# A hybrid decoder trunk in float32: the GLA gate inputs stacked as high and low parts on partitions, and the gate logits formed by two rounded products

## The chip, the cores and the metric

The kernel runs on one core of one Trainium2 chip. The metric is device time of one execution in microseconds (us); lower is better. The engines are named as the profile names them: PE is TensorE (matrix products, with PEld its weight loads), DVE is VectorE, ACT is ScalarE, POOL is GpSimd, SP is SyncE, which here only issues DMAs. POOL issues DMAs too.

## The reference, cut to what matters

One layer with three branches that read the same normalised rows. Only the gated linear attention (GLA) branch is touched by the change, and of it only the forget gate:

```python
h = rmsnorm(x, norm_gain)
proj = h @ w_in                                   # one combined projection
q, k, v, gla_g, a_lr, u, pool_g, xq, xg, merge = jnp.split(proj, split_pts, axis=-1)
z = (a_lr @ w_a2 + b_a).astype(jnp.float32)       # a_lr: (B, T, 16), w_a2: (16, 512)
log_a = (jax.nn.log_sigmoid(z) / GATE_TAU).reshape(B, T, GLA_HEADS, GLA_DK)
o, S = gla_chunked(q, k, v, log_a, S0)            # 4 heads of key width 128
```

There are 1024 prompt rows and 8 sample rows. The gate input a_lr has rank 16 and the logits z have 512 columns, 128 for each of the four heads. All tensors are float32.

## The kernel before

The order of the work on PE and of the DMAs that SP issues is that of the program text. The instructions of ACT, DVE and POOL are put in order when the kernel is compiled, by a scheduler with a cost model of its own; on the chip each engine then runs its list in that fixed order.

**The main stream.** The combined projection is cut into 36 pairs of column blocks. A pair is worked as seven products; each is 2 column halves x 4 inner steps x 3 matmuls of 128x258 (`product`, with `mm3` at L242 to L244). mm3 multiplies float32 operands as high part times high part, high times low and low times high, all in the rounded type fp32r; ACT makes the high part (L223) and DVE the low part (L224). After the pairs come 24 units of the branch projections and then the output projection.

**The side stream.** After every half of a product `fill` takes steps from generators: first the memory projection, then cross attention (`cross_steps`, 16 steps of `s` and two to drain), then GLA (`gla_steps`, 16 chunks of 256 columns), then pooling. Each `yield` carries a cost by which the side work is spread over the main stream, so that PE always has something to run.

**The gate.** `small_loads` fetches the 16 columns of w_in that give a_lr into `wa`, which has 32 columns of which 16 were set to zero, and copies w_a2 four times into `w2`, 128x512, at partitions 32j to 32j+15. `gate_half` multiplies `wa` with the normalised rows into four groups of 32 output partitions, one group for every fourth inner block, so that its 128 partitions hold four partial sums of a_lr. They go to DRAM (`al_scr`) for the prompt and into `als` for the samples. Later `gla_load` fetches a chunk of them as `alc`, and one plain float32 matmul of `w2` with `alc` adds the four partial sums and multiplies by w_a2 at once (L907, 16 times; L1012 for the samples, 4 times):

```python
nc.tensor.matmul(t[:, :CT], lhsT=w2[:, h * P:(h + 1) * P], rhs=alc, start=True, stop=True)
gate_exps(t[:, :CT], CT, h, z, b)
```

**What sets the order around the change.** Three stores of buffers matter. `R` gives 2 KB tiles from a ring of 14 (`NR`) that nearly all small work shares: cross attention's queries, their high parts, probabilities `p`, transposed probabilities `pT`, outputs `xo`, memory tiles. `E` gives 30 (`NE`) larger tiles, 28 of which hold the operands of the main stream during the pairs. `PX` and `PZ` are PSUM tiles of the main and side stream. In cross attention, step s runs `cross_scores(s)`, then `cross_values(s-2)`, then `cross_weights(s-1)`, so that what a step makes is used one step later. POOL's list holds the stores of results to DRAM: `xo` at L737, `c` at L593 with the copy of the sample columns at L569 before it, `mkv` at L457 and L458.

Of the kernel before, what the change touches and what calls it, by code (L numbers as in the profile page):

```python
# [9 lines left out]
F32 = mybir.dt.float32  # L10
F32R = mybir.dt.float32r
# [3 lines left out]
AF = mybir.ActivationFunctionType  # L15
ALU = mybir.AluOpType
AX = mybir.AxisListType

P = 128
D = 1024  # L20
T = 1024
NS = 8
# [25 lines left out]
def trunk_kernel(ctx: ExitStack, tc: tile.TileContext,  # L48
# [65 lines left out]
    def R(shape, dt=F32, name="r"):  # L114

        return shaped(wk.tile([P, 512], dt, tag="ring", name=name, bufs=NR), shape)
# [68 lines left out]
    nc.vector.memset(pm, 0.0)  # L185
    qm = pm[:, 0]

    w2 = cp.tile([P, 512], F32, name="w2")
    nc.vector.memset(w2, 0.0)
    ssq = cp.tile([P, 16], F32, name="ssq")  # L190
    nc.vector.memset(ssq, 1.0)

    smp = cp.tile([P, 33 * NS], F32, name="smp")
    brs = [cp.tile([P, NK, NS], F32, name=f"brs{n}") for n in range(3)]
    als = cp.tile([P, NS], F32, name="als")
    S_XQ, S_Q, S_K, S_V, S_U = 0, 8, 12, 16, 24

    def smp_of(j, n=1):
# [2 lines left out]
    def scratch(n, name, shape):  # L201
        return [dr.tile(list(shape), F32, name=f"{name}{i}") for i in range(n)]
# [3 lines left out]
    acc_scr = [scratch(NK, f"acc{n}_", (P, TT)) for n in range(2)]  # L206
    mkv_scr = [scratch(NH, f"mkvs{o}", (P, 2, DV)) for o in range(2)]
    al_scr = scratch(2, "als", (P, HT))
    q_scr, k_scr = (scratch(2, s, PAIR) for s in ("qsc", "ksc"))
    vt_scr = scratch(NH, "vtsc", (T, DV))  # L210
    u_scr, xq_raw = (scratch(4, s, PAIR) for s in ("usc", "xqsc"))
# [22 lines left out]
    def split_in(x, shape, name, scale=None):  # L234

        hi, lo = R(shape, F32R, name + "h"), x.bitcast(F32R)
        split(hi, lo, x, scale)
        return hi, lo
# [35 lines left out]
        nc.sync.dma_start(out=x_t[tb], in_=x_p[tb * P:(tb + 1) * P, :])  # L274

    wa = R([NK, 32], name="wa")
    nc.vector.memset(wa, 0.0)

    def small_loads():
        nc.gpsimd.dma_start(out=wa[:, :, :GATE], in_=w_in[:, O_A:O_A + GATE].rearrange("(k p) n -> p k n", p=P))  # L280
        for j in range(4):
            nc.gpsimd.dma_start(out=w2[32 * j:32 * j + GATE], in_=w_a2)


    ORDER = (2, 0, 1)
# [382 lines left out]
    def loaded(src, shape, name, alloc=None):  # L668
        t = (alloc or R)(shape, name=name)
        nc.sync.dma_start(out=t, in_=src)  # L670
        return t
# [22 lines left out]
    def cross_fetch(h, c):  # L694
        cross["xq", h, c] = loaded(chunk_of(xq_raw[h], c), [2, CT], "xq")
# [136 lines left out]
    def cross_steps():  # L832
        def scores(n):
            cross_scores(n // 4, n % 4)

        def memory(n):
            if n % 4 == 0:
                cross_memory(n // 4)

        def weights(n):  # L840
            cross_weights(n // 4, n % 4)

        def values(n):
            cross_values(n // 4, n % 4)

        samples = chain_of(cross_sample(h) for h in range(NH))
        cross_load(0)
        cross_memory(0)
        cross_fetch(0, 0)
        yield 2  # L850
        cross_queries(0, 0)
        cross_fetch(0, 1)
        for s in range(16 + 2):
            if s < 16:
                scores(s)
                yield 3
                if s + 1 < 16:
                    cross_queries(*divmod(s + 1, 4))
                if s + 2 < 16:
                    cross_fetch(*divmod(s + 2, 4))  # L860
            if s % 4 == 2 and s < 14:
                cross_load(s // 4 + 1)
            if s >= 1:
                yield next(samples, 0)
            if 0 <= s - 2:
                values(s - 2)
                yield 1.7
            if s >= 1:
                yield next(samples, 0)
            if s % 4 == 3 and s < 15:  # L870
                memory(s + 1)
                yield 2
            if 0 <= s - 1 < 16:
                weights(s - 1)
                yield 1.7
            for _ in range(3):
                if s >= 1:
                    yield next(samples, 0)
        yield from samples
# [8 lines left out]
    def gate_exps(t, w, h, z, m):  # L888
# [4 lines left out]
        act(z, z, AF.Ln, bias=one_c)  # L893
        nc.vector.tensor_tensor(m, m, z, op=ALU.subtract)

    def gla_load(h, c):
        alc = wk.tile([P, CT], F32, tag="alc", name="alc", bufs=2)
        nc.sync.dma_start(out=alc, in_=al_scr[c // 2][:, (c % 2) * CT:(c % 2 + 1) * CT])
        kq = R([2, CT], name="kq")
        for j, scr in enumerate((k_scr, q_scr)):  # L900
            nc.sync.dma_start(out=kq[:, j], in_=scr[h // 2][:, 2 * (h % 2) + c // 2, (c % 2) * CT:(c % 2 + 1) * CT])
        gla["in", h, c] = alc, kq

    def gla_gates(h, c):
        alc, kq = gla["in", h, c]
        t = PZ()
        nc.tensor.matmul(t[:, :CT], lhsT=w2[:, h * P:(h + 1) * P], rhs=alc, start=True, stop=True)  # L907
        bz = R([2, CT], name="bz")
        b, z = bz[:, 0], bz[:, 1]
        gate_exps(t[:, :CT], CT, h, z, b)  # L910
        nc.vector.tensor_tensor_scan(b, smask, b, 0.0, op0=ALU.mult, op1=ALU.add)
        bl = b.rearrange("p (c e t) -> p c e t", e=2, t=64)[:, :, :, 63]
        dec = wk.tile([P, 4], F32, tag="dec", name="dec", bufs=3)
        d2 = dec.rearrange("p (c e) -> p c e", e=2)
        act(d2, bl, AF.Exp, scale=1.0 / TAU)
        decp = wk.tile([P, 2], F32, tag="decp", name="decp", bufs=3)
        nc.vector.tensor_tensor(decp, d2[:, :, 0], d2[:, :, 1], op=ALU.mult)
        blp = wk.tile([P, 4], F32, tag="blp", name="blp", bufs=2)
        blp2 = blp.rearrange("p (c e) -> p c e", e=2)
        nc.vector.tensor_copy(blp2[:, :, 1], bl[:, :, 1])  # L920
        nc.vector.tensor_tensor(blp2[:, :, 0], bl[:, :, 0], bl[:, :, 1], op=ALU.add)
        k, q = kq[:, 0], kq[:, 1]
        kiqi = R([2, CT], name="kiqi")
        ki, qi = kiqi[:, 0], kiqi[:, 1]
        act(z, b, AF.Exp, scale=1.0 / TAU, bias=lnq_c)
        nc.vector.tensor_tensor(q, q, z, op=ALU.mult)
        q4, qi4 = (x.rearrange("p (a e t) -> p a e t", e=2, t=64) for x in (q, qi))
        nc.vector.tensor_copy(qi4[:, :, 0], q4[:, :, 0])
        nc.vector.tensor_tensor(qi4[:, :, 1], q4[:, :, 1], d2[:, :, 0:1].to_broadcast([P, 2, 64]), op=ALU.mult)
        act(z, b, AF.Exp, scale=-1.0 / TAU)  # L930
        nc.vector.tensor_tensor(ki, k, z, op=ALU.mult)
        nc.vector.tensor_tensor(z.rearrange("p (c t) -> p c t", t=64), blp[:, :, None].to_broadcast([P, 4, 64]),
                                b.rearrange("p (c t) -> p c t", t=64), op=ALU.subtract)
        act(z, z, AF.Exp, scale=1.0 / TAU)
        nc.vector.tensor_tensor(k, k, z, op=ALU.mult)
        gla["g", h, c] = kq, kiqi, decp
# [69 lines left out]
    def gla_sample(h):  # L1006
# [2 lines left out]
            gla_rows(0)  # L1009
            yield 1  # L1010
        t = PZ()
        nc.tensor.matmul(t[:, :NS], lhsT=w2[:, h * P:(h + 1) * P], rhs=als, start=True, stop=True)  # L1012
        z, m = tiny(NS, "gz"), tiny(NS, "gm")
        gate_exps(t[:, :NS], NS, h, z, m)
        dec = wk.tile([P, NS], F32, tag="as", name="as", bufs=2)
# [550 lines left out]
```

## Time and profile before

| | |
|---|---|
| time, median of 3 runs | 1442.38 us (1441.68 to 1443.36) |
| the profiled execution's own time | 1445.01 us |
| its span from first to last instruction | 1443.3 us |
| mean granted TensorE clock | 0.997 |
| DVE busy | 916.2 us (63%) |
| ACT busy | 679.0 us (47%) |
| POOL busy | 222.1 us (15%) |
| bytes moved by DMA | 259.42 MB, mean 180 GB/s |

Busy time counts an engine's own instructions; DMA issues on SP are not in it. Matmuls are pipelined: a row of 0.28 us does not hold PE for 0.28 us, and what one costs in a full stream is read from the distance of starts. The plain float32 matmul shows as two MATMUL records with two weight loads.

### The profile page before, as it was taken

The numbers are of one execution on the slowest core, as the hardware profiler recorded it, in microseconds if no ns is written. First come the engines' busy times: TensorE is split into PE (matmuls) and PEld (weight loads), VectorE is DVE, ScalarE is ACT, GpSimd is POOL, SyncE is SP. The second block draws the span as 40 slices with busy tenths as digits, with TensorE's granted clock in tenths as the row PEclk, the third lists the DMA queues.
The fourth block names the chain that finished last, engine by engine and source line by source line (L and its number), as shares of the span: only waits on it lengthen the run. The fifth ranks groups of instructions, "written<-read, shape, count | busy, mean of one in ns | idle before, by whom it ended". The sixth has DMA issues, their size and how long they took to land.

```text
span 1443.3 us, 28179 instructions
## 1 busy us (share of the span) xinstructions
PE 1417.4 (98%) x10689; PEld 1356.1 (94%) x10689; DVE 916.2 (63%) x2123; ACT 679.0 (47%) x1575; POOL 222.1 (15%) x401
## 2 busy tenths in 40 slices
PE   8999999999999999999999999999999999999998
PEld 6899999989899999999999999999999999999876
DVE  6954756666687777767766778785672434554436
ACT  6743544443465666656654445444472432233212
POOL 3211111124342121212221111111010000000000
PEclk9999999999999999999999999999999999999999
DMA  9355665656656363554654455454694777632633
GB/s 329 125 165 169 217 218 187 207 175 165 198 155 193 115 192 129 182 176 126 187 167 150 149 188 170 159 184 163 204 298 134 234 257 249 234 104 79 224 118 116
DMA packets 183507, 259.42 MB, mean 180 GB/s; under 512 B 22204, under 2 KB 132564, under 8 KB 183364
## 3 DMA queue, kind: packets, MB, share of 16 engines
q1 hardware_dynamic: 159900, 183.87, 41.5%
q0 software_dynamic: 23328, 73.56, 14.7%
q8 instruction: 84, 1.38, 0.4%
q14 instruction: 51, 0.42, 0.1%
q10 hardware_dynamic: 144, 0.20, 0.0%
HBM read 180.47 MB, written 77.56 MB: 179 GB/s over the span
## 4 chain that ended last, share of the span: by engine, by line
PE 88%; DMA 5%; DVE 5%; issue 1%; ACT 1%; SPq 0%; POOL 0%; DVEq 0%; ACTq 0%; POOLq 0%
PE px L242 25%; PE px L243 25%; PE px L244 25%; DMA qb<-xqs 3%; PE pz L244 2%; PE pz L243 2%; PE pz L242 2%; DMA raw<-in_w_in_dram 1%; DVE kc L777 1%; PE pz L963 1%; PE pz L404 1%; PE pz L944 1%; PE pz L817 1%; PE pz L946 1%; PE pz L907 0%
## 5 line engine op out<-in xcount | busy, mean ns | idle before, releaser
L244 PE MATMUL px<-bh,wbl 128*128 128x384 f32 (+1 forms) x576 | 184.1, 320 | 0.0
L243 PE MATMUL px<-bl,wbh 128*128 128x384 f32 (+1 forms) x576 | 184.1, 320 | 0.0
L242 PE MATMUL px<-bh,wbh 128*128 128x384 f32 (+1 forms) x576 | 183.7, 319 | 0.0
L554 ACT ACTIVATE r<-px 128x258 f32<-128x258 f32 x240 | 89.9, 375 | 47.4 <-PE px L244 46.9
L242 PEld LDWEIGHTS px<-bh,wbh 128*128 128x128 f32 x576 | 108.3, 188 | 0.0
L243 PEld LDWEIGHTS px<-bl,wbh 128*128 128x128 f32 x576 | 108.2, 188 | 0.0
L244 PEld LDWEIGHTS px<-bh,wbl 128*128 128x128 f32 x576 | 108.2, 188 | 0.0
L242 PE MATMUL px<-ot,s1h 128*128 128x258 f32 x320 | 94.1, 294 | 0.0
L242 PE MATMUL px<-o,a12h 128*128 128x258 f32 x320 | 93.4, 292 | 0.0
L242 PE MATMUL px<-ot,s3h 128*128 128x258 f32 x320 | 93.2, 291 | 0.0
L242 PE MATMUL px<-o,s4h 128*128 128x258 f32 x320 | 93.0, 291 | 0.2 <-DVE c L636 0.2
L242 PE MATMUL px<-o,a11h 128*128 128x258 f32 x320 | 92.8, 290 | 0.0
L242 PE MATMUL px<-ot,a22h 128*128 128x258 f32 x320 | 92.6, 289 | 0.0
L242 PE MATMUL px<-ot,s2h 128*128 128x258 f32 x320 | 92.2, 288 | 0.0
L243 PE MATMUL px<-o,a11h 128*128 128x258 f32 x320 | 91.1, 285 | 0.3 <-DVE o L224 0.3
L243 PE MATMUL px<-o,a12h 128*128 128x258 f32 x320 | 91.1, 285 | 0.0
L244 PE MATMUL px<-o,a12l 128*128 128x258 f32 x320 | 91.0, 284 | 0.0
L244 PE MATMUL px<-ot,s1l 128*128 128x258 f32 x320 | 90.9, 284 | 0.0
L243 PE MATMUL px<-ot,s1h 128*128 128x258 f32 x320 | 90.8, 284 | 0.0
L244 PE MATMUL px<-o,a11l 128*128 128x258 f32 x320 | 90.6, 283 | 0.0
L243 PE MATMUL px<-ot,s2h 128*128 128x258 f32 x320 | 90.1, 281 | 0.5 <-DVE ot L224 0.5
L243 PE MATMUL px<-ot,a22h 128*128 128x258 f32 x320 | 90.5, 283 | 0.0
(471 smaller groups left out, 4634.3 us busy)
## 6 DMA issues: line engine op xcount, KB each, us to landing
raw<-in_w_in_dram SPq DMA_DIRECT2D x80, 512.0 KB, 4.0
msc<-c POOLq DMA_DIRECT2D x24, 516.0 KB, 4.8
brsc<-c POOLq DMA_DIRECT2D x24, 516.0 KB, 3.7
sig<-msc SPq DMA_DIRECT2D x24, 516.0 KB, 6.0
brr<-brsc SPq DMA_DIRECT2D x48, 256.0 KB, 5.2
wbr<-in_w_branch_dram SPq DMA_DIRECT2D x24, 512.0 KB, 5.5
acc<-sig POOLq DMA_DIRECT2D x16, 516.0 KB, 5.2
acc<-acc SPq DMA_DIRECT2D x16, 516.0 KB, 7.0
```

The costliest lines, as they stand in the source:

```text
L242: nc.tensor.matmul(out, lhsT=lh, rhs=rh, start=start, stop=False, skip_group_check=more)
L243: nc.tensor.matmul(out, lhsT=lh, rhs=rl, start=False, stop=False, skip_group_check=more)
L244: nc.tensor.matmul(out, lhsT=ll, rhs=rh, start=False, stop=stop, skip_group_check=more)
L404: nc.tensor.matmul(t[:, :DV], lhsT=memT[k // 2][:, k % 2, a * P:(a + 1) * P], rhs=raw[k // 2][:, k % 2], start=k == 0, stop=k == NK - 1)
L554: nc.scalar.activation(r, acc[c][:, :QT], AF.Copy)
L777: nc.vector.tensor_tensor_reduce(kc[:, a, :], kc[:, a, :], qb[:, bb, :], scale=1.0, scalar=0.0, op0=ALU.mult, op1=ALU.add, accum_out=sc[:, ...
L817: nc.tensor.matmul(t[32 * j:32 * j + 32, :DV], lhsT=pm[:, a, 4 * i + j, :], rhs=vc[j][:, a, :], start=a == 0, stop=a == 1)
L944: nc.tensor.matmul(t[0:64, 0:P], lhsT=ki[:, 0:64], rhs=qi, start=True, stop=True)
L946: nc.tensor.transpose(t[:, P:2 * P], kt, ident)
L963: nc.tensor.matmul(to, lhsT=kiqi[:, 1, cs], rhs=st, start=False, stop=True)
```

## The change

The gate weights `wa` get a second copy of their 16 columns where the zeros were, so the four groups of 32 partitions each hold a_lr's partial sum twice. From the identity matrix two columns per partition are made: `second_copy` is 1 on the second copy's partitions and 0 elsewhere, `copy_sign` is +1 on the first copy and -1 on the second. `gate_inputs` then turns a tile of partial sums x into one that holds the rounded high part on the first copy's partitions and the remainder, x minus its rounded part, on the second's. `gate_weights` fetches w_a2 eight times, on every 16 partitions, splits it into a high and a low part and stores both for each head in DRAM (`w2_scr`). `gla_load` fetches a head's two parts when it loads the head's first chunk. The logits are then two fp32r matmuls, high weights and low weights, each with the stacked input; together they hold all four products of parts.

`gate_weights` runs in step s = 6 of cross attention, `gate_inputs` in steps 7 and 8. The four loads of `w2` at the start and two memsets go.

```diff
-    w2 = cp.tile([P, 512], F32, name="w2")
-    nc.vector.memset(w2, 0.0)
+    gm = cp.tile([P, 4], F32, name="gm")
+    nc.vector.tensor_reduce(gm[:, 0:2], ident.rearrange("p (j e r) -> p e j r", j=4, e=2), axis=AX.XY, op=ALU.add)
+    nc.vector.tensor_tensor(gm[:, 2:3], gm[:, 0:1], gm[:, 1:2], op=ALU.subtract)
+    second_copy, copy_sign = gm[:, 1:2], gm[:, 2:3]
...
+    als_parts = cp.tile([P, NS], F32R, name="alsp")
...
+    alp_scr = scratch(2, "alps", (P, 512))
+    w2_scr = scratch(NH, "w2s", (P, 2, P))
...
     wa = R([NK, 32], name="wa")
-    nc.vector.memset(wa, 0.0)
 
     def small_loads():
         nc.gpsimd.dma_start(out=wa[:, :, :GATE], in_=w_in[:, O_A:O_A + GATE].rearrange("(k p) n -> p k n", p=P))
-        for j in range(4):
-            nc.gpsimd.dma_start(out=w2[32 * j:32 * j + GATE], in_=w_a2)
+        nc.gpsimd.tensor_copy(wa[:, :, GATE:], wa[:, :, :GATE])
...
+            if s == 6:
+                gate_weights()
+            elif s in (7, 8):
+                gate_inputs(s - 7)
...
+    def gate_weights():
+        w = R([NH, P], name="w2")
+        for j in range(8):
+            nc.gpsimd.dma_start(out=w[16 * j:16 * j + GATE], in_=w_a2.rearrange("r (h n) -> r h n", h=NH))
+        hi, lo = split_in(w, [NH, P], "w2")
+        for j, x in enumerate((hi, lo)):
+            for h in range(NH):
+                nc.gpsimd.dma_start(out=w2_scr[h][:, j], in_=x[:, h].bitcast(F32))
+
+    def gate_inputs(i):
+        def stacked(hi, x):
+            nc.scalar.activation(hi, x, AF.Copy, scale=copy_sign)
+            nc.gpsimd.tensor_scalar(x, x, second_copy, None, op0=ALU.mult)
+            nc.gpsimd.tensor_tensor(hi, hi.bitcast(F32), x, op=ALU.add)
+
+        if i == 0:
+            stacked(als_parts, als)
+        hi = R([512], F32R, "al")
+        stacked(hi, loaded(al_scr[i][:, :512], [512], "alr"))
+        nc.gpsimd.dma_start(out=alp_scr[i], in_=hi.bitcast(F32))
+
     def gla_load(h, c):
-        alc = wk.tile([P, CT], F32, tag="alc", name="alc", bufs=2)
-        nc.sync.dma_start(out=alc, in_=al_scr[c // 2][:, (c % 2) * CT:(c % 2 + 1) * CT])
+        if c == 0:
+            wg = gla["w2", h] = wk.tile([P, 2, P], F32R, tag="w2s", name="w2s", bufs=2)
+            nc.sync.dma_start(out=wg.bitcast(F32), in_=w2_scr[h])
+        alc = wk.tile([P, CT], F32R, tag="alc", name="alc", bufs=2)
+        nc.sync.dma_start(out=alc.bitcast(F32), in_=alp_scr[c // 2][:, (c % 2) * CT:(c % 2 + 1) * CT])
...
-        nc.tensor.matmul(t[:, :CT], lhsT=w2[:, h * P:(h + 1) * P], rhs=alc, start=True, stop=True)
+        for j in range(2):
+            nc.tensor.matmul(t[:, :CT], lhsT=gla["w2", h][:, j], rhs=alc, start=j == 0, stop=j == 1)
...
-        nc.tensor.matmul(t[:, :NS], lhsT=w2[:, h * P:(h + 1) * P], rhs=als, start=True, stop=True)
+        for j in range(2):
+            nc.tensor.matmul(t[:, :NS], lhsT=gla["w2", h][:, j], rhs=als_parts, start=j == 0, stop=j == 1)
```

## The prediction

> **What bounds the kernel now.** I read the page's busy shares and its chain of work first, then the busy time by stretches, then the rows of the gate matmuls.
>
> ```profile
> PE 1417.4 (98%) x10689; PEld 1356.1 (94%) x10689; DVE 916.2 (63%) x2123; ACT 679.0 (47%) x1575; POOL 222.1 (15%) x401
> PE 88%; DMA 5%; DVE 5%; issue 1%; ACT 1%; SPq 0%; POOL 0%; DVEq 0%; ACTq 0%; POOLq 0%
> 0.00:36.00 36.00, 28.83 (x165) 23.66 (x169) 23.51 (x58) 22.41 (x46) 11.20 (x38) 1.00 0.98 329
> 200.00:220.00 20.00, 20.00 (x170) 20.00 (x169) 12.53 (x37) 7.50 (x18) 2.52 (x5) 1.00 0.84 274
> 220.00:240.00 20.00, 20.00 (x171) 19.90 (x169) 16.63 (x45) 12.17 (x31) 3.17 (x6) 1.00 0.53 166
> 300.00:375.00 75.00, 69.05 (x579) 65.57 (x578) 43.94 (x110) 28.28 (x67) 25.70 (x42) 0.98 0.62 179
> 500.00:700.00 200.00, 200.00 (x1635) 191.17 (x1634) 148.07 (x392) 123.78 (x348) 40.70 (x68) 1.00 0.53 166
> ```
>
> A row of stretches gives length, then busy time of PE, PEld, DVE, ACT and POOL, the granted clock, the DMA share and GB/s. PE is busy 98% of the span and carries 88% of the chain. It idles 7.2 us in the first 36 us, where DMA is 98% busy, and 6 us in 300 to 375, inside cross attention. From 500 to 700, GLA, it never idles: there the kernel is as long as PE's work, and a matmul made shorter shortens it, so long as nothing new makes PE wait.
>
> **The gates on PE.** Columns: start, duration, what.
>
> ```profile
> L907 PE MATMUL pz<-alc,w x32: 377/378/382, 381.1 to 699.1; 128*128 128x256 f32 x32
> L1012 PE MATMUL pz<-als,w x8: 170/214/256, 411.6 to 686.9; 128*128 128x8 f32 x8
> ...
> 380.97 0.28 PE L244 MATMUL px<-o,a11l 128*128 128x258 f32 x1
> 381.10 0.59 PE L907 MATMUL pz<-alc,w 128*128 128x256 f32 x2
> 381.34 0.47 PE L242 MATMUL px<-o,s4h 128*128 128x258 f32 x1
> 381.64 0.28 PE L243 MATMUL px<-o,s4h 128*128 128x258 f32 x1
> ...
> 383.92 0.28 PE L244 MATMUL px<-o,s4l 128*128 128x258 f32 x1
> ```
>
> The 0.377 us of a row is not its cost, because rows overlap; starts are. From 381.64 to 383.92 lie 19 steps of the ordinary stream, 0.120 us each. From 380.97 to 381.64 lie 0.67 us, in which PE takes two ordinary matmuls (0.24) and the gate. So the plain float32 gate costs 0.43 us; 16 of them run, all between 381 and 699 us.
>
> What replaces it, two fp32r matmuls of 128x256, has its like in the scores of cross attention:
>
> ```profile
> 201.60 0.28 PE L242 MATMUL pz<-mkTh,xqsh 128*128 128x256 f32 x1
> ...
> 203.02 0.28 PE L242 MATMUL px<-o,a11h 128*128 128x258 f32 x1
> ```
>
> Twelve such matmuls, each with a weight load of its own, lie between those starts: 1.42 / 12 = 0.118 us. Two cost 0.237. The gain is 0.43 - 0.24 = 0.19 us a gate, **16 x 0.19 = 3.0 us**. It is certain to about 0.2 us, since starts are read to 0.01 us.
>
> [...]
>
> The sample gates have only 8 columns:
>
> ```profile
> 411.45 0.28 PE L244 MATMUL px<-ot,a22l 128*128 128x258 f32 x1
> 411.57 0.28 PE L1012 MATMUL pz<-als,w 128*128 128x8 f32 x2
> 411.71 0.36 PE L242 MATMUL px<-ot,a22h 128*128 128x258 f32 x1
> 411.91 0.28 PE L243 MATMUL px<-ot,a22h 128*128 128x258 f32 x1
> ```
>
> By the same reckoning one costs 0.46 - 0.24 = 0.22 us for two records with two weight loads. After the change there are again two records with two loads, at most the 0.237 us of the wide pair. So each lies between 0.22 won and 0.02 lost, four of them between -0.9 and +0.1 us; I take 0, since the row itself already has two loads and hardly any columns.
>
> **The start.** Four DMA issues of w2 go, and two memsets, which end before DVE's first copy out of PSUM. A POOL copy of wa's 16 columns comes in behind wa's landing.
>
> ```profile
> wa<-in_w_in_dram POOLq DMA_DIRECT2D x1, 64.0 KB, 7.7
> w<-in_w_a_dram POOLq DMA_DIRECT2D x4, 32.0 KB, 7.0
> 5.66 0.94 POOL L280 DMA_DIRECT2D wa<-in_w_in_dram  x1
> 15.03 0.59 POOL L457 DMA_DIRECT2D out_dram<-mkv  x1 [6.08 <-DVE mkv L408]
> 18.32 11.94 DMA raw<-in_w_in_dram
> L1391 POOL COPY mgs<-zeros 128x128 f32<-128x128 f32 x2 | 3.3, 1654 | 3.8 <-DVE bl L224 3.8
> L520 PE MATMUL pz<-h,wa x64: 378/381/406, 33.8 to 51.9; 128*32 128x258 f32 x64
> ```
>
> wa lands by about 5.66 + 0.94 + 7.7 = 14.3 us. A POOL copy of the same 128 elements took 1.65 us, so the new one ends by 16 us, where the first store of mkv is put back by about 1 us at most, and the first matmul with wa starts at 33.8: hidden. The chain waits 11.94 us for the first projection weights while the DMAs move 329 GB/s; 4 x 32 KB less is 0.4 us at that rate. What it wins is 0 (if those weights did not queue behind them) to 0.4 us; I take 0.2. ACT work follows them on the chain, so the whole need not arrive.
>
> **What is added at s = 6 to 8.** By the stores of xo at 209.84 (step 6) and 225.18 (step 7) this lies at about 201 to 245 us.
>
> ```profile
> 209.84 0.67 POOL L737 DMA_DIRECT2D mixsc<-xo  x1 [7.29 <-ACT xo L736]
> 225.18 0.68 POOL L737 DMA_DIRECT2D mixsc<-xo  x1 [11.20 <-ACT xo L736]
> L282 POOL DMA_DIRECT2D w<-in_w_a_dram x4 | 2.0, 496 | 0.4 <-DMA rows<-in_norm_gain_dram 0.4
> L223 ACT ACTIVATE mvsh<-mkv 128x512 fp32r<-128x512 f32 x4 | 2.5, 624 | 0.0
> L224 DVE TENSOR_TENSOR mkv<-mkv,mvsh 128x512 fp32r<-128x512 f32 x4 | 2.7, 682 | 0.0
> POOL mixsc L737 <- ACT xo L736: 75.1, 11, 14.3
> ```
>
> ACT gets three 512-wide copies (0.62 each) and a tiny one: 2 us. DVE gets one subtraction, 0.7 us. POOL gets 8 loads and 8 + 2 stores at 0.5 to 0.7 us, some 10 us, and four 512-wide operations that the trace has no like of; between the 0.2 us of a small copy and four times the 1.65 us above each, they cost 1 to 26 us, and I take some 7, by the 128-wide copy. Of these 40 us POOL is busy 5.7, and it mostly waits for xo, so its own 17 us fit. SP gets two loads of 256 KB and later four of w2s, beside 16 fetches of alc that stay. PE gets nothing.
>
> The cover is that PE was never idle from 200 to 240 us, with DVE busy 12.5 and 16.6 of 20 us. Queued behind POOL's waits (for the loads of w, for the split) are the stores of c and xo; behind ACT's two kinds of loads are the copies that free PSUM for the main stream; behind SP's two loads, if they wait for a ring tile, are the next projection weights. I cost all of it at 0 in the forecast, with 0 and 7 us as ends, worked out with the rivals.
>
> **Sum.** 3.0 + 0 + 0.2 = 3.2 us less. Against the profiled execution: 1445.01 - 3.2 = 1441.8, its span 1443.3 - 3.2 = 1440.1, the 1.7 us around it unchanged. That execution lies 2.6 us over the median of the runs shown; from the median, 1442.38 - 3.2 = **1439.2 us**. Its own range, with the gates' 0.2, the start's 0 to 0.4 and the samples' bounds, is 1437.9 to 1439.7.
>
> **Rivals.**
>
> *Part is given back through the ring.* The ring of 14 is nearly full in step 6: by the program some 12 tiles are held when xo is made (memory parts 4, raw memory 2, queries 3, probabilities 2, xo 1), and the transposed probabilities make 13 or 14. gate_weights holds 2 more from its loads to its last store, gate_inputs 2 in each of its steps. That a full ring reaches PE is seen later in the trace:
>
> ```profile
> 302.08 5.67 DMA mixsc<-xo
> 307.84 0.10 DVE pTl L224
> 308.68 1.07 PE pz L817 x16
> PE pz L803 <- DVE ps L798: 2.4, 1, 2.4
> PE pz L243 <- DVE pTl L224: 1.5, 1, 1.5
> ```
>
> A store of xo has to land before pTl gets its tile, and PE waits 1.5 us. Against it stands that a step's results are needed a step, some 15 us, later. One such wait of 1.5 to two of 2.4 would give 1440.7 to 1444.0, around 1441.6 (one of 2.4).
>
> *ACT stands still before a load; the kernel gets slower.* ACT's list is fixed when compiling. If the high part of w2 stands in it by an optimistic landing, ACT waits, and the copies of r and c behind it hold the accumulators. Between a half product's end and the next use of its accumulator PE has three half products, 36 x 0.12 = 4.3 us, less the copy of 0.4: a wait under about 4 us is hidden. Eight issues and a landing of 7.0 us are 8 x 0.5 + 7.0 = 11 us from the first issue, so the wait's excess is at most 7 us and the time at most 1439.2 + 7 = 1446.2; with an excess of 6.5, 1445.7. The decisive point for slower is an excess of some 6 us. For it: ACT waited for loads elsewhere, up to 5.0 us at once. Against it: those in GLA were 1.5 at the longest, and a compiler that knows of DMA latency puts the split late.
>
> ```profile
> ACT sig L75 <- DMA sig<-msc: 35.9, 15, 5.0
> ACT s L1030 <- DMA s<-in_state_gla_dram: 11.0, 10, 1.5
> ```
>
> [...]
>
> *The other waits of cross attention shift.* New orders of ACT, DVE and POOL after step 6 can also shorten waits: PE idles 6 us from 300 to 375. A third to a half of that more is 1436.2 to 1437.2.
>
> *It does not do what it says.* If two fp32r matmuls with stacked operands cost PE what the plain one did, there is no gain: about 1442.2. Against it stand the twelve score matmuls.
>
> **How the numbers follow.** A measurement of this kernel can tell about 0.2%, 2.9 us, from no change, so the bound for faster is 1439.5 and the forecast lies just beyond it. Forecast 0.42 (0.33 faster, 0.09 same); ring 0.29 (same); ACT 0.12 (0.10 slower, 0.02 same); shifted waits 0.12 (faster); no gain 0.05 (same). That is faster 0.45, same 0.45, slower 0.10. The range runs from 1436.8, which leaves out the far half of the shifted waits, to 1444.5, which leaves out the ACT rival.
>
> **What would show it.** Right: 32 fp32r rows at the gates, and 0.24 us of PE instead of 0.43 between neighbours; PE busy the whole of 200 to 245; the first projection weights landing 0.2 us earlier. Ring: a wait of PE on pTl, mkTl or xo between 205 and 250 with a DMA on the chain before it. ACT: a wait of ACT on the load of w or alr over 4 us, with PE's px waiting for r or c. Wrong altogether: PE idle time in 300 to 500 that differs from before by more than 3 us, in either direction, since no step of mine puts it there.

## The result, and the profile after

| | before | changed |
|---|---|---|
| median | 1443.28 us (8 runs, 1439.78 to 1445.42) | 1450.99 us (8 runs, 1446.08 to 1455.54) |
| ratio changed / before | | 1.0055, 95% interval 1.004 to 1.007 |
| the profiled execution's own time | 1445.01 us | 1450.49 us |
| its span | 1443.3 us | 1448.1 us |
| mean granted clock | 0.997 | 0.994 |

The changed kernel is 7.7 us slower by the medians, and the interval lies wholly above 1. Between the two profiled executions the difference is 5.5 us, because that of before lies above its median. What follows compares these two traces, so its sum is about 5 us; the verdicts of the experiments are ratios of medians.

The page of the changed kernel: busy time of the engines, then the shares of the chain of work.

```profile
PE 1417.7 (98%) x10689; PEld 1356.0 (94%) x10689; DVE 917.9 (63%) x2124; ACT 680.4 (47%) x1579; POOL 244.5 (17%) x422
PE 89%; DVE 4%; DMA 3%; issue 1%; ACT 1%; SPq 1%; POOL 0%; DVEq 0%; ACTq 0%; POOLq 0%
```

Nothing stands out here. PE's busy time is the same to 0.3 us although about 3 us of matmuls were taken away, which already says that PE took 3 us longer over something else. The busy times by stretches (length, PE, PEld, DVE, ACT, POOL, clock, DMA share, GB/s) say where:

```profile
220.00:240.00 20.00, 16.20 (x114) 15.56 (x114) 13.69 (x35) 6.75 (x16) 5.73 (x7) 0.83 0.54 169
240.00:260.00 20.00, 18.21 (x144) 15.84 (x143) 9.22 (x17) 7.78 (x21) 5.10 (x6) 1.00 0.66 211
300.00:375.00 75.00, 68.11 (x577) 65.56 (x576) 48.87 (x126) 29.51 (x72) 26.72 (x44) 1.00 0.63 178
500.00:700.00 200.00, 200.00 (x1650) 191.33 (x1649) 149.76 (x403) 124.76 (x350) 37.51 (x63) 1.00 0.53 162
```

From 220 to 240 us PE did 114 matmuls where it did 171 before. It was idle for 3.8 us of that, and the granted clock was 0.83. It was idle 1.8 us more in the next 20. GLA, 500 to 700, is as full as before and holds 15 more matmuls.

**The gates gained what was forecast.** The group of the gates by its source line, first and last start in it:

```profile
L939 PE MATMUL pz<-alc,w2s x32: 274/281/364, 389.0 to 704.4; 128*128 128x256 f32 x32
```

The first of them on PE's timeline (start, duration, what):

```profile
389.04 0.39 PE L939 MATMUL pz<-alc,w2s 128*128 128x256 f32 x2
389.27 0.28 PE L247 MATMUL px<-o,s4h 128*128 128x258 f32 x1
```

From 389.04 to 389.27 lie 0.23 us for the pair. The first and last gate are 315.4 us apart; before they were 381.1 to 699.1, 318.0 us. So 2.6 us were won between them, over 15 gates, 0.17 us each.

**The loss lies in cross attention.** The same instruction can be found in both traces (its line number is 3 higher in the changed kernel here); how much later it runs is the loss so far. From the chain of work of before (start, duration, what):

```profile
211.77 0.44 PE pz L724 x4
...
232.07 0.22 PE pz L791 x2
...
244.60 1.00 PE pz L817 x16
```

The chain of the changed kernel:

```profile
209.25 0.44 PE pz L727 x4
...
219.19 5.66 DMA alr<-als
224.96 0.73 ACT al L914
225.78 0.70 POOL alr L915
...
227.32 4.88 DMA mixsc<-xo
...
233.50 0.63 PE pz L794 x2
...
236.71 0.21 PE pz L247
...
246.59 5.76 DMA vc<-in_cache_mem_v_dram
252.40 1.05 PE pz L820 x10
```

At 209 us the changed kernel is 2.5 us ahead. At the two transposes of the sample scores (L794) it is 1.4 us late: 3.9 us lost. At the end of the sample value matmuls (L820) it is about 8 us late, and the first gate is 389.0 - 381.1 = 7.9 us late. From there the gates bring it to 704.4 - 699.1 = 5.3. So cross attention lost 2.5 + 7.9 = 10.4 us, nearly all of it between 210 and 254 us. The waits of PE from 200 to 262 us (total, times, longest):

```profile
PE pz L794 <- DVE sc L780: 3.5, 1, 3.5
PE pz L820 <- DMA vc<-in_cache_mem_v_dram: 1.5, 1, 1.5
```

Before, PE has no wait at all in this stretch. The chain is read like this. ACT reaches the copy of `alr` (L914) too early and stands still before its load; the copy that makes `xo` is behind it. ACT's timeline, the idle time before an instruction and its releaser in brackets:

```profile
224.96 0.72 ACT L914 ACTIVATE al<-alr,gm 128x512 fp32r<-128x512 f32 x1 [4.59 <-DMA alr<-als]
225.59 0.58 ACT L739 ACTIVATE xo<-pz 128x512 f32<-128x512 f32 x1
```

POOL's timeline:

```profile
225.78 1.57 POOL L915 TENSOR_SCALAR alr<-alr,gm 128x512 f32<-128x512 f32 x1 [6.46 <-ACT al L914]
227.32 0.71 POOL L740 DMA_DIRECT2D mixsc<-xo  x1
227.99 1.37 POOL L916 TENSOR_TENSOR al<-al,alr 128x512 fp32r<-128x512 f32 x1
```

DVE's timeline:

```profile
227.57 2.35 DVE L229 TENSOR_TENSOR a12l<-raw,a12h 128x512 fp32r<-128x512 f32 x1
...
232.32 0.69 DVE L229 TENSOR_TENSOR pTl<-pz,pTh 128x512 fp32r<-128x512 f32 x1 [0.78 <-DMA mixsc<-xo]
232.93 0.41 DVE L780 CUSTOM_DVE_ANT_0 kc<-kc,qb 128x256 f32<-128x256 f32 x1
```

`xo` is stored at 227.3 instead of 225.2, the store lands at 232.2, and only then does `pTl` get a tile: the ring of 14 is full. The transposes of the samples' scores, which PE runs at a fixed place of its list, wait for two things. They take a PSUM tile, of which the side stream has two (`PZ`, `bufs=2` in the kernel); by the order of the program the one they take held the transposed probabilities last, so `pTl` must have read it. And they read the sums of the last dot products (`kc`, L780), which in the changed kernel stand behind `pTl` on DVE's list. `pTl` ends at 232.32 + 0.69 = 233.0 and the transposes start at 233.5, so the dot products add at most 0.5 us; the rest of PE's 3.5 us is the wait for `pTl` itself. Before, DVE and PE ran at this place:

```profile
229.68 0.69 DVE L224 TENSOR_TENSOR pTl<-pz,pTh 128x512 fp32r<-128x512 f32 x1
231.91 0.38 PE L791 MATMUL pz<-ident,sc 128*8 128x128 f32 x2
```

`pTl` ended there at 230.4, 1.5 us ahead of the transposes. That was its slack.

Two more costs come in. In the chain the matmuls after 234 us come 0.21 us apart instead of 0.12 until about 239.5, which adds some 2.5 us. And SP issues the loads of the samples' values (`vc`) 8 us later than before (the changed kernel's timeline of SP), behind the load of `xq` and the new one of `alr`:

```profile
239.30 0.53 SPq L673 DMA_DIRECT2D xq<-xqsc  x1
243.51 0.34 SPq L673 DMA_DIRECT2D alr<-als  x1
...
244.37 2.76 SPq L673 DMA_DIRECT2D vc<-in_cache_mem_v_dram  x4
```

The same loads on SP's timeline before:

```profile
236.40 2.04 SPq L670 DMA_DIRECT2D vc<-in_cache_mem_v_dram  x4
```

Of the 8 us, 4.1 are of `xq` (issued at 235.17 before), which waits for a matmul of PE and so comes behind PE's delay. The other 3.8 are of `alr`: its issue stands 3.6 us, by the kernel for a tile of the ring, until a matmul of the values frees one (the chain goes from PE L249 at 243.48 to SP). This part does not follow from PE's wait at the transposes. In inputs_here below that wait is only 0.4 us, and SP still stands 3.7 us between `xq` (230.53) and `alr` (234.71), with PE waiting 2.2 us for `vc`.

PE, by its timeline, stands before `vc` and then takes the 16 matmuls as the loads come in:

```profile
248.50 0.28 PE L249 MATMUL px<-ot,s2l 128*128 128x258 f32 x1
250.29 3.15 PE L820 MATMUL pz<-vc,pm 128*32 128x256 f32 x16 [1.52 <-DMA vc<-in_cache_mem_v_dram]
253.38 0.39 PE L247 MATMUL px<-ot,s2h 128*128 128x258 f32 x1
```

From 248.50 to 253.38 are 4.9 us for what took 1.0 + 0.12 before: 3.7 us lost. The three terms, 3.9 + 2.5 + 3.7 = 10.1, make up the 10.4 of the loss but for 0.3 us.

### The profile page after: what moved, and what is told of

The parts are those of the page before. It is cut to its first block, busy times and chain, and to the rows that moved or that the text cites. A ratio compares the mean times of both kernels' runs of the same rounds, so it can differ in the third digit from the quotient of the medians.

```text
span 1448.1 us, 28238 instructions
## 1 busy us (share of the span) xinstructions
PE 1417.7 (98%) x10689; PEld 1356.0 (94%) x10689; DVE 917.9 (63%) x2124; ACT 680.4 (47%) x1579; POOL 244.5 (17%) x422
## 4 chain that ended last, share of the span: by engine, by line
PE 89%; DVE 4%; DMA 3%; issue 1%; ACT 1%; SPq 1%; POOL 0%; DVEq 0%; ACTq 0%; POOLq 0%
PE px L247 26%; PE px L248 25%; PE px L249 25%; PE pz L249 2%; PE pz L248 2%; PE pz L247 2%; DMA qb<-xqs 1%; PE pz L995 1%; PE pz L976 1%; PE pz L820 1%; DVE kc L780 1%; DMA x<-in_x_prompt_dram 1%; PE pz L978 1%; PE pz L407 0%; DMA vc<-in_cache_mem_v_dram 0%
## 5 line engine op out<-in xcount | busy, mean ns | idle before, releaser
L249 PE MATMUL px<-bh,wbl 128*128 128x384 f32 (+1 forms) x576 | 184.1, 320 | 0.0
L249 PEld LDWEIGHTS px<-bh,wbl 128*128 128x128 f32 x576 | 108.2, 188 | 0.0
L247 PE MATMUL px<-ot,s1h 128*128 128x258 f32 x320 | 93.6, 292 | 0.0
L247 PE MATMUL px<-o,s4h 128*128 128x258 f32 x320 | 93.0, 291 | 0.2 <-DVE c L639 0.2
L247 PE MATMUL px<-ot,a22h 128*128 128x258 f32 x320 | 92.2, 288 | 0.0
L249 PE MATMUL px<-o,a12l 128*128 128x258 f32 x320 | 91.0, 284 | 0.0
L249 PE MATMUL px<-o,s4l 128*128 128x258 f32 x320 | 90.8, 284 | 0.0
L248 PE MATMUL px<-o,s4h 128*128 128x258 f32 x320 | 90.6, 283 | 0.0
L249 PE MATMUL px<-ot,s1l 128*128 128x258 f32 x320 | 90.6, 283 | 0.0
L249 PE MATMUL px<-o,a11l 128*128 128x258 f32 x320 | 90.6, 283 | 0.0
```

The source lines that it names most:

```text
L247: nc.tensor.matmul(out, lhsT=lh, rhs=rh, start=start, stop=False, skip_group_check=more)
L248: nc.tensor.matmul(out, lhsT=lh, rhs=rl, start=False, stop=False, skip_group_check=more)
L249: nc.tensor.matmul(out, lhsT=ll, rhs=rh, start=False, stop=stop, skip_group_check=more)
```

## The experiments

All were timed in five rounds beside the kernel before, so that the ratios, not the single times, are to be compared. Every edit is against the changed kernel. In the texts on record, A is the order of the new work in the lists of ACT and POOL, B the ring of 14, and C, formed on the way, that whatever delays the samples' chain through the fixed lists of DVE, ACT and SP at that place costs the same, whichever resource does it.

**prep_only: the preparation stays, the gates are plain float32 again.** `w2` is loaded at the start as before, and the prepared parts are not used.

```diff
...
-        for j in range(2):
-            nc.tensor.matmul(t[:, :CT], lhsT=gla["w2", h][:, j], rhs=alc, start=j == 0, stop=j == 1)
+        nc.tensor.matmul(t[:, :CT], lhsT=w2[:, h * P:(h + 1) * P], rhs=alc, start=True, stop=True)
...
```

> All of the preparation at steps 6 to 8 stays, and the gates are again one plain float32 product (w2 loaded at the start as before; the prepared parts are not used). Theory A (the preparation costs some 10 us at steps 6 to 8 and the gates give back 3): no gain between 381 and 699 us, a loss of 8 to 11 us against before, ratio 1.006 to 1.008, and the same wait of PE of about 3.5 us near 230 us. Rival (the two rounded products themselves cost the time): within 2 us of before.

1452.95 us, ratio 1.0071 (1.0056 to 1.0087). PE's first wait from 150 to 262 us (line numbers are 5 higher here):

```profile
PE pz L799 <- DVE sc L785: 3.3, 1, 3.3
```

The wait and the loss are there without the products. Its first gate starts at 391.9 us and its last at 710.0, 10.8 and 10.9 us later than before: the plain gates give nothing back. So the products bring their gain, 2.6 us, and the preparation takes away some four times as much.

**no_stack: the stacking is left out.** `alp_scr` is filled by a copy from DRAM to DRAM, `als_parts` by one small ACT copy; the split of w2 stays.

```diff
-            stacked(als_parts, als)
-        hi = R([512], F32R, "al")
-        stacked(hi, loaded(al_scr[i][:, :512], [512], "alr"))
-        nc.gpsimd.dma_start(out=alp_scr[i], in_=hi.bitcast(F32))
+            nc.scalar.activation(als_parts, als, AF.Copy, scale=copy_sign)
+        nc.gpsimd.dma_start(out=alp_scr[i], in_=al_scr[i][:, :512])
```

> gate_weights and the two rounded products stay; the stacking of the inputs is left out (they are copied from DRAM to DRAM, no ACT, POOL or SP work, no ring tile). Theory A1 (it is the input part at steps 7 and 8: ACT and POOL stand before the load of alr, and the store of xo behind it): no wait of 3 us near 230 us, granted clock 1.00 there, 3 to 5 us faster than before, ratio 0.996 to 0.998. Rival A2 (the two ring tiles that gate_weights holds for 20 us, or its 16 DMAs): the wait near 230 us stays, ratio over 1.003.

1440.91 us, ratio 0.999 (0.9979 to 1.0001). PE still waits 1.3 us at the transposes, now with `pTl` itself as the releaser, but the clock from 220 to 240 us is 1.00 and `vc` comes in time. Most of the loss hangs on the stacking, by its work or by its tiles, and not on moving its bytes, which the copies here still do.

**dve_op and prefetch: the order on POOL, and on ACT.** The first puts one DVE operation in the place of POOL's two; the second loads `alr` one step earlier, so that ACT doesn't wait for it.

```diff
-            nc.gpsimd.tensor_scalar(x, x, second_copy, None, op0=ALU.mult)
-            nc.gpsimd.tensor_tensor(hi, hi.bitcast(F32), x, op=ALU.add)
+            nc.vector.scalar_tensor_tensor(hi, x, second_copy, hi.bitcast(F32), op0=ALU.mult, op1=ALU.add)
```

> The two POOL operations of the stacking become one DVE operation. In the trace of the changed kernel the store of xo of step 5 stands behind the first POOL operation (1.57 us) and DVE is held 1.7 us during the second. Theory A1 with POOL as the main part: the store of xo goes out 1.5 to 2 us earlier, PE's wait falls from 3.5 to 1 to 2 us and the clock may stay at 1.00: 3 to 6 us faster than the changed kernel. If ACT's wait of 4.6 us for the load is the main part: the wait stays over 2.5 us and the time within 2 us of the changed kernel's 1451.

1451.79 us, ratio 1.0064 (1.0046 to 1.0082). The store of xo goes out at 226.43, 0.9 us earlier than in the changed kernel, and lands no earlier (232.6 against 232.2), since it took 6.19 us instead of 4.88. PE waits 4.0 us. Nothing won.

```diff
+            if s in (6, 7):
+                gate_fetch(s - 6)
...
+    def gate_fetch(i):
+        gla["alr", i] = loaded(al_scr[i][:, :512], [512], "alr")
...
-        stacked(hi, loaded(al_scr[i][:, :512], [512], "alr"))
+        stacked(hi, gla["alr", i])
```

> alr is loaded one step earlier, all else as in the changed kernel. If ACT's wait for the load is the main part: ACT waits under 1 us, xo of step 5 is made some 4 us earlier, PE's wait near 230 us is gone or under 1 us, 6 to 9 us faster than the changed kernel (1441 to 1445). If the ring is the main part (alr holds its tile a step longer): no better, or slower than 1451.

1452.57 us, ratio 1.0078 (1.006 to 1.0095). Its chain at that place holds:

```profile
227.44 5.19 DMA alps<-al
```

ACT no longer stops before the load (it waits 2.1 us for the landing of a store of xo instead) and `xo` is made 2.6 us earlier, but now `pTl` waits for the store of `al`, which holds the other tile that the ring is short of. PE waits 4.1 us. The edit also keeps the tile of `alr` a step longer, so it doesn't test the order with the ring as it was. Still, repairing either queue alone wins nothing: each time the next tile to come free takes up the gain, and the order (A) is not the whole cause.

**no_ring and ring_only: the tiles without the work, and the work without the tiles.** no_ring stacks in four pieces of 256 columns, in buffers of `alc` and `w2s` that stand empty then, so that the stacking takes no tile of the ring. ring_only does no stacking but takes its two tiles in each of the two steps, from a load by SP to a store by POOL.

```diff
-        hi = R([512], F32R, "al")
-        stacked(hi, loaded(al_scr[i][:, :512], [512], "alr"))
-        nc.gpsimd.dma_start(out=alp_scr[i], in_=hi.bitcast(F32))
+        for c in range(2):
+            cs = slice(c * CT, (c + 1) * CT)
+            hi = wk.tile([P, CT], F32R, tag="alc", name="al", bufs=2)
+            x = wk.tile([P, 2, P], F32, tag="w2s", name="alr", bufs=2).rearrange("p a b -> p (a b)")
+            nc.sync.dma_start(out=x, in_=al_scr[i][:, cs])
+            stacked(hi, x)
+            nc.gpsimd.dma_start(out=alp_scr[i][:, cs], in_=hi.bitcast(F32))
```

> The stacking keeps its loads, its ACT copies and its two POOL operations, but works in four pieces of 256 columns on two 1 KB buffers each that stand empty until GLA starts; no ring tile is held by alr and al. Theory B (in step 7 the ring is full and the low part of the transposed probabilities waits on DVE for the landing of a store that frees a tile; the two tiles of the stacking are what fills it): DVE does not wait before pTl near 230 us, PE's wait there is under 1 us, the clock stays 1.00, 1438 to 1442. Theory A1 (the waits of ACT for the load and POOL's operations ahead of the store of xo): those are still there, in more pieces, so PE still waits 2 to 4 us and the time is 1447 to 1453.

```diff
...
+        x = [loaded(al_scr[i][:, :512], [512], "alr") for _ in range(2)]
+        for j in range(2):
+            nc.gpsimd.dma_start(out=alp_scr[i], in_=x[j])
```

> No stacking on ACT or POOL: two ring tiles are loaded by SP in each of steps 7 and 8 and stored by POOL as they are. Theory B: holding the two tiles from load to landing is enough, PE waits 2 to 4 us near 230 us with pTl behind the landing of a store, the clock falls, 1446 to 1453. Theory A1: without ACT and POOL work nothing stands before the store of xo, PE does not wait there, 1439 to 1443 like the kernel without the stacking.

no_ring: 1448.45 us, ratio 1.0036 (1.0023 to 1.0049). ring_only: 1453.07 us, ratio 1.0071 (1.0057 to 1.0086). The chain of ring_only, the last dot product on its DVE, and PE's wait:

```profile
225.84 7.35 DMA alps<-alr
...
233.48 0.70 DVE pTl L229
...
234.23 0.58 PE pz L794 x2
```

```profile
231.47 0.42 DVE L780 CUSTOM_DVE_ANT_0 kc<-kc,qb 128x256 f32<-128x256 f32 x1
PE pz L794 <- DVE pTl L229: 5.0, 1, 5.0
```

Here all dot products are done at 231.9, before `pTl`, and PE still waits until `pTl` ends: the transposes need `pTl` itself, by their PSUM tile. Tiles held in the place of the stacking make the whole loss without any of its wide operations. The test is not a pure one: `gate_weights` still works in step 6, both tiles are held from load to landing, which the stacking does with neither, and twice the bytes move. Freeing the stacking's tiles, in turn, gives back only 1.0055 - 1.0036 = 0.0019, some 2.7 us, and the two intervals overlap: the two tiles of `gate_weights` are still in the ring, and PE still waits 2.9 us at the transposes and 2.0 us for `vc`. There `pTl` waits for no tile; it stands behind dot products for which DVE waited 2.4 us, until 230.99, for their load `qb`. So neither "ring" nor "work" has it alone, which is where C comes from.

**no_ring_dve: no_ring and the DVE operation together.**

> As no_ring, and the two POOL operations are one DVE operation. Theory B: no wait near 230 us either; the DVE's four operations of 0.4 us are hidden, 1438 to 1441, within 2 us of no_ring. Theory A1: PE waits still 2 us or more for ACT behind its loads, 1446 or more.

1449.55 us, ratio 1.0044 (1.003 to 1.0059), not to be told from no_ring. The wait at the transposes is 2.2 us instead of 2.9, that for `vc` 2.4 instead of 2.0.

**early: the whole preparation in another place.** Six pieces of 256 columns (two for the weights, four for the inputs) run in the memory projection, at every third of its 16 steps (about 50 to 112 us), in the buffers of no_ring, with SP's loads and the DVE operation. The products and the amount of preparation are the same, but besides the place four things differ from the change: the width of the pieces, the buffers, the DVE operation, and SP as the issuer of the loads of w_a2.

```diff
+            if n % 3 == 0:
+                gate_piece(n // 3)
...
-            if s == 6:
-                gate_weights()
-            elif s in (7, 8):
-                gate_inputs(s - 7)
...
+    def gate_piece(n):
+        hi = wk.tile([P, CT], F32R, tag="alc", name="gph", bufs=2)
+        x = wk.tile([P, 2, P], F32, tag="w2s", name="gpx", bufs=2).rearrange("p a b -> p (a b)")
+        if n < 2:
+            for j in range(8):
+                nc.sync.dma_start(out=x[16 * j:16 * j + GATE], in_=w_a2[:, n * CT:(n + 1) * CT])
...
```

> The whole preparation, weights too, moves out of cross attention into the memory projection (about 70 to 110 us), in six pieces of 256 columns on the buffers that GLA uses later, with one DVE operation for the stacking; the gates stay two rounded products. Theory C (what costs time is that the preparation delays the serial chain of the samples in cross attention, whose kc and qb loads, DVE dot products and PE transposes have no slack; the gates themselves give 3 us): no wait over 1.5 us near 230 us, clock 1.00 there, 3 to 5 us faster than before, ratio 0.996 to 0.998. Rival (any place costs as much, since the added 30 DMAs and splits collide somewhere): 1445 or more.

**1436.88 us, ratio 0.9967 (0.9953 to 0.998): faster than both kernels.** Two of the stretches in which the changed kernel lost:

```profile
220.00:240.00 20.00, 20.00 (x173) 19.54 (x176) 15.29 (x37) 10.44 (x26) 3.86 (x7) 1.00 0.61 200
240.00:260.00 20.00, 20.00 (x183) 18.78 (x176) 8.68 (x18) 8.06 (x20) 1.60 (x3) 1.00 0.50 160
```

PE has no wait from 150 to 262 us. So the preparation can be had without the loss; what of that is its place and what its form is told apart by spread_sp below. The 0.0033 over the kernel before are 4.8 us, of which the gates give 2.6; where the other 2 come from is open.

**weights_s2: only the weights moved, to step 2.**

```diff
-            if s == 6:
+            if s == 2:
                 gate_weights()
```

> Only gate_weights moves, from step 6 to step 2; the stacking stays at 7 and 8 on the ring. If the two ring tiles and the DMAs of gate_weights in step 6 are what starts the delay of the sample chain: PE's wait near 230 us falls from 3.5 to under 2 us, clock 1.00 there, 1441 to 1446. If the stacking alone is enough: the wait stays 3 us or more with the clock low after it, 1448 to 1453.

1457.48 us, ratio 1.0101 (1.0079 to 1.0123), worse by 0.0046. Its chain:

```profile
150.04 5.29 DMA w<-in_w_a_dram
...
155.51 0.63 ACT w2h L228
...
156.41 0.50 ACT xo L739
...
156.95 0.58 PE pz L247
157.53 0.21 PE pz L248
```

Here ACT stands still 3.7 us before the split of w2, its copies of c and xo are behind it, and PE waits 4.3 us: the forecast's rival of ACT, in the open, in a place where the changed kernel doesn't have it. After that wait, too, the matmuls come at 0.21 us. Another wait of 3.9 us follows at the sample transposes of the head before (177.8 us), for `mkTl`. At the transposes where the change waits 3.5 us, 0.9 are left, so taking the weights out of step 6 did help there. The wait for `vc` stays, with 2.2 us.

**spread_no_ring and spread_sp: six small pieces in cross attention, no tile of the ring.** One piece in each of steps 3 to 8; in the first POOL loads w_a2, in the second SP.

```diff
+            if 3 <= s <= 8:
+                gate_piece(s - 3)
```

> The whole preparation stays in cross attention but holds no ring tile: six pieces of 256 columns, one a step from step 3 to 8, one DVE operation for the stacking. Theory B (ring tiles alone): no wait over 1.5 us before 250 us, 1438 to 1442. Theory C with queues (ACT, DVE, POOL and SP work in these steps delays the sample chain without any ring tile): waits of 2 us or more at the sample transposes, 1444 to 1450.

1458.38 us, ratio 1.0107 (1.0086 to 1.0129): spoilt by something else. Its timeline of POOL at the start:

```profile
6.62 2.03 POOL L906 DMA_DIRECT2D gpx<-in_w_a_dram  x4
...
12.85 3.83 POOL L906 DMA_DIRECT2D gpx<-in_w_a_dram  x8
```

The scheduler put the loads of w_a2, which wait for nothing, near the head of POOL's list, and a split with them ahead of most of DVE's copies of `memT`: PE waited 12.0 us for `memT`, and the products with `wa` start at 49.8 us instead of 33.8. Up to the first gate (398.3 us) it falls back only some 1.2 us more, but the weights are no longer prepared in cross attention here, so this says little of the two theories.

> Like spread_no_ring (steps 3 to 8, no ring tile, one DVE operation), but w_a2 is loaded by SP in the program's order, so that nothing of it is moved to the start of the kernel, where spread_no_ring lost 16 us. If holding ring tiles is what makes cross attention slow: no wait over 1.5 us between 150 and 260 us, 1438 to 1442. If the added work on ACT, DVE and SP in these steps is enough: waits of 2 us or more, 1444 or more.

1443.14 us, ratio 1.0007 (0.9994 to 1.0019). The start is as in the changed kernel, PE waits no longer than 0.4 us at the transposes, and 2.9 us in three parts for `vc` (in an execution 4 us above the median). Against the change, with no tile of the ring, small pieces and one DVE operation, 1.0055 - 1.0007 = 0.0048 is gone, over half of the 0.0088 that lie between the change and early. Against early nothing differs but the place and the spacing of the pieces: 1.0007 - 0.9967 = 0.004, 5.8 us, is their price with no tile of the ring in it.

**inputs_here and weights_here: which half costs what.** In the first the weights are prepared early and the inputs stay in steps 7 and 8; in the second the reverse. inputs_here, then weights_here:

```diff
+            if n in (0, 3):
+                gate_piece(n // 3)
...
-            if s == 6:
-                gate_weights()
-            elif s in (7, 8):
+            if s in (7, 8):
                 gate_inputs(s - 7)
...
```

```diff
+            if n in (6, 9, 12, 15):
+                gate_piece(n // 3)
...
             if s == 6:
                 gate_weights()
-            elif s in (7, 8):
-                gate_inputs(s - 7)
...
```

> The weights are prepared early (memory projection, no ring tile); the stacking stays in steps 7 and 8 on the ring as in the change. If the stacking alone makes the wait near 230 us: PE waits 2.5 us or more there with the clock low, 1445 to 1450. If it needs both parts to pass the point where the clock drops: the wait stays under 2 us, 1437 to 1442.

> The stacking is done early; gate_weights stays in step 6 on the ring as in the change. By the kernel without the stacking (1440.9, a wait of 1.3 to 1.6 us near 230 us): 1439 to 1442, that is 2 to 4 us over the early version, with the clock at 1.00.

| in cross attention | median, us | ratio to before | over early |
|---|---|---|---|
| nothing (early) | 1436.88 | 0.9967 (0.9953 to 0.998) | |
| weights (weights_here) | 1441.23 | 0.9995 (0.9984 to 1.0006) | 0.0028, 4.0 us |
| inputs (inputs_here) | 1444.54 | 1.0021 (1.001 to 1.0032) | 0.0054, 7.8 us |
| both (the change) | 1450.99 | 1.0055 (1.004 to 1.007) | 0.0088, 12.7 us |

The last column is the difference of the ratios, times 1443 us. The halves add up to 11.8 of the 12.7 us, within what the intervals allow. With the weights alone PE waits 2.3 us for `pTl` at the transposes; with the inputs alone it waits 0.4 us there and 2.2 us for `vc`. In these two traces the clock stays 1.00 from 220 to 260 us, where the change has a wait of 3.5 us and half the clock behind it. Both traces are of the fastest execution of their kernel, though (1439.37 and 1441.18 us), with a mean clock of 0.999; most other executions have 0.995 to 0.998, so their loss may well hold slow clock too.

## Why the prediction was wrong

Forecast 1439.2 us, range 1436.8 to 1444.5; measured 1450.99.

- **The gates: right.** 0.237 us forecast for the pair, 0.23 measured; 0.19 gained each, 0.17 measured over 15. "It does not do what it says" is out: prep_only lacks just this gain.
- **The start: right in sign, small in size.** Forecast 0.2 (0 to 0.4) us ahead; the changed trace is 1.3 ahead at the last product with `wa` (50.6 against 51.9 us). The cause is open, as all kernels of the study but spread_no_ring were 0.8 to 2.0 us ahead there, prep_only with its loads of w2 kept among them (0.9).
- **POOL's four wide operations: right.** Forecast some 7 us; a pair takes 1.57 + 1.37, two pairs 5.9. They fitted into POOL's idle time as forecast, and that didn't matter.
- **"What is added at s = 6 to 8 ... I cost all of it at 0": this step failed.** It cost 10.4 us in the traces, and even the upper end, 7, was short. Its cover, "PE was never idle from 200 to 240 us", was a statement about PE and not about the chain that feeds it. The row of PE tells that its operands came in time, not by how much. What counted was the slack of what the sample transposes need: `pTl`, which has to clear their PSUM tile and was done 1.5 us ahead before, the dot products on DVE, and SP's issue of `vc` behind the new load.
- **The ring rival: right in mechanism and place, wrong in size.** The landing of a store of xo releases `pTl`, then PE, as in the chain quoted for it from 302 us. It was priced at one wait of 1.5 us to two of 2.4. Measured were 3.9 us at the transposes, 2.5 of slow clock and 3.7 in the late `vc`. The two prices were not of the quoted chain: that one ends in a wait of 1.0 us, for `pm`, which stands behind `pTl` on DVE; the 1.5 us lie at 356 us, and the 2.4 are a wait for `ps`, at 366. Only waits were priced: the slow clock behind them and the ring's hold on SP's list were not followed. And its main objection, that results are needed a step later, is true of the values of `pTl`, but not of the PSUM tile that `pTl` has to read.
- **The ACT rival: seen, not deciding.** ACT waited 4.6 us for `alr`, above the 4 us that were to be hidden, and PE didn't wait for r or c. Taking that wait away (prefetch) won nothing. weights_s2 shows that the rival is real elsewhere.
- **The shifted waits: seen, and small.** Before, PE waits 1.0 us for `mkTl` at 169 us; the changed kernel doesn't. From 300 to 375 us PE is idle 6.9 us instead of 6.0.

Shown: the preparation in cross attention makes the loss, and the products don't (prep_only, early); its place alone, without any tile of the ring, costs 5.8 us (spread_sp against early); tiles held in the place of the stacking make the whole loss without its work (ring_only). Not settled: how the 10.4 us divide between tiles and queues in the changed kernel itself, because each removal lets the other come through. A ring of more than 14 tiles, a third PSUM tile for the side stream, and the change's own form in the early place were not tried.

## What to carry to other kernels

A busy engine is cover only if the chain that feeds it has slack; look for the instruction with the fixed place (here two transposes), list all it needs, its output buffer too, follow back which in-order lists each of these passes, and ask what the new work puts ahead of it there. A buffer of a shared ring that is held until a store lands keeps the next taker, and everything behind that taker, for that long: 4.9 to 7.4 us from issue to landing in the rows above. When a preparation depends on nothing late, try it where nothing waits for the lists: in the same form it cost 5.8 us less some 140 us earlier, and 12.7 us less than the change with its ring tiles.

## What the runs showed of the hardware

**After a wait of 3.5 us the granted clock fell to 0.50.** In stretches of 2 us of the changed kernel it was:

```profile
232.00:234.00 2.00, 0.50 (x3) 0.34 (x4) 1.68 (x6) 0.00 (x0) 0.49 (x1) 0.61 0.71 270
234.00:236.00 2.00, 2.00 (x11) 2.00 (x11) 1.65 (x4) 0.28 (x1) 0.00 (x0) 0.50 0.02 6
...
238.00:240.00 2.00, 2.00 (x14) 2.00 (x14) 0.96 (x3) 0.00 (x0) 0.00 (x0) 0.69 0.00 0
```

Half the clock for some 6 us, in which PE counts as fully busy and does 11 to 14 matmuls in 2 us instead of 2 / 0.12 = 17. Across the study the clock from 220 to 240 us was 1.00 with a wait of 2.3 us (weights_here), 0.91 with 2.2 (no_ring_dve), 2.9 (no_ring), 3.3 (prep_only), 4.1 (prefetch) and 5.0 (ring_only), 0.83 with 3.5 and 4.0 (the change, dve_op); where the wait came late, part of the slow time may lie behind 240. From 240 to 260 us it was 0.91 with waits for `vc` of up to 2.0 us (no_ring) and 2.1 us (no_ring_dve), and 1.00 with one of 2.2 us (inputs_here). So the length of one wait doesn't decide alone; no run here tests what does.

**DVE was slow beside an operation of POOL.** The subtraction of `a12l`, 0.69 us at the median of its 40 rows in the changed kernel, took 2.35 us at 227.57 (timeline above), while POOL's two-input operation ran from 227.99 for 1.37 us: 1.7 us more. Beside the second of these operations on a wide tile, at 249.74 us for 1.33, a DVE row of L308 took 2.08 us (249.54), where the median of that group's 80 rows is 0.69. Both times DVE's row starts before POOL's. No run here tests what holds DVE up.
